# One VectorE operation a step and column in the block inverse of a gated-DeltaNet layer, with a second set of buffers, later transpositions and the decay product on VectorE

## The chip, the cores and the metric

The kernel runs on one core of one Trainium2 chip, in one launch. The metric is the device time of that launch in microseconds (us). Three runs of the kernel before took 2078.45, 2078.91 and 2074.31 us, median 2078.45. A fourth execution was taken with the hardware profiler: 2073.93 us, of which 2072.0 us are the span of its instructions. All durations below come from that execution.

## The reference, cut to what matters

One decoder block on 256 tokens of width 2048: a feed-forward part (SwiGLU, inner width 5632), a mixer, a second feed-forward part, a gated embedding and a last normalisation. The mixer is eight gated-DeltaNet heads of width 128 and sixteen state-space heads that share one input and one output projection. The change touches two places of it. The first is the inverse of a unit lower triangular matrix of each head and chunk; the second is the product of the state-space heads' decay with `cb`.

```python
lower = jnp.where(strict, jnp.einsum('bnhik,bnhjk->bnhij', kb, k) * decay, 0.0)
t_inv = lax.linalg.triangular_solve(eye + lower, eye, left_side=True, lower=True)
u = jnp.einsum('bnhij,bnhjv->bnhiv', t_inv, v * beta[..., None])
...
cb = jnp.einsum('bnlgd,bnsgd->bngls', cc, bc)
y_diag = jnp.einsum('bngrls,bnsgrp->bnlgrp', cb[:, :, :, None] * seg, xc)
```

## The kernel before, in words

**Matrix products.** Each weight tile is 128 x 2048 in float32. A DMA on SP's queue loads it (`raw`, three buffers), ScalarE casts 1024 columns of it to a rounded half `hi` (line 118), VectorE takes the rest `lo = raw - hi` (line 119), and TensorE multiplies both with the split activations. `hi` and `lo` have four buffers each. In the mixer every 1024 columns are 24 matmuls of 256 columns (lines 145 to 147: `hi` with the upper half of the activations, `hi` with the lower, `lo` with the upper). So TensorE needs one `hi` and one `lo` for each 24 matmuls, and the `lo` of VectorE stand in VectorE's one queue among all its other work.

**The mixer.** 52 input tiles (`win`) come in the order: four pairs of DeltaNet heads (k, q, v) with the state-space keys and inputs between them, then the gates z of the state-space heads, then the gates of the four DeltaNet pairs. Then 16 tiles of the output projection (`wout`) follow, which multiply `osp`, the split outputs of all heads. A gate tile pair i is multiplied into pair i's result `oT` at line 886, and casts to `osp` (lines 195 and 196) feed the output projection.

**Side work.** Everything of the heads beside the projections is written as generators (`gdn_pair`, `ssd_quad`) that go one `yield` further after each 1024 columns (`tick`). `WAIT` and `STEP` count such yields. This is only the order in which instructions are recorded; a scheduler then lays them out per engine, and every engine runs its list strictly in order.

**One pair of heads (`gdn_pair`).** Two heads and two chunks of 128 tokens make four 128 x 128 matrices. Their sixteen 32 x 32 diagonal blocks are inverted by substitution on VectorE (lines 656 to 665). Four DMAs on POOL's queue take the blocks to DRAM (line 630), one DMA on SP's queue spreads each block over eight partitions (`Lb`, line 632), and each partition solves four columns `Z`. Each of 31 steps j is two operations over all four columns: `tb` = row of L times Z's element j (line 663), then Z minus `tb` (line 665). Then `Z` goes to DRAM and back as `Y` (lines 666 and 671, POOL's queue), VectorE transposes it (line 674), and two levels of matmuls merge the blocks: `ip`, `ix`, `iy` (line 685). After them comes a chain: `y`, `st`, `o`, `ks` and `qs`, `y`, `o` (line 714), each separated by a copy on ScalarE or VectorE; then the squares on ScalarE (745), eight small POOL operations for the inverse root (747 to 751 with 220 to 225), the scaling (753), the transpositions `ot` (758) and the copy to `oT` (759). Pairs share `Lb`, `Z`, `tb`, `qs` and `o`, which have one buffer each.

**The state-space heads (`ssd_quad`).** For each of four quads POOL multiplies the decay, in two operations of 128 x 512, with `CB` (line 820). `py` (line 832) waits for that.

Of the kernel before, what the change touches and what calls it, by code (L numbers as in the profile page):

```python
# [9 lines left out]
F32 = mybir.dt.float32  # L10
F32R = mybir.dt.float32r
AF = mybir.ActivationFunctionType
ALU = mybir.AluOpType
PSUM = bass.MemoryType.PSUM

P = 128
# [27 lines left out]
BS = 32  # L44
CG = 4
# [4 lines left out]
WAIT = 4  # L50
# [18 lines left out]
def tile_hybrid_block(ctx, tc, xT, pT, con, par, wgu1, wd1, wnar, win, wout, wgu2, wd2, wproj, wple, outT):  # L69
    nc = tc.nc  # L70
    act, dve, pool, pe = nc.scalar, nc.vector, nc.gpsimd, nc.tensor
# [25 lines left out]
    def over(ap, n):  # L97
        return ap.unsqueeze(1).to_broadcast([ap.shape[0], n, ap.shape[-1]])
# [263 lines left out]
    with ExitStack() as mix:  # L362
# [213 lines left out]
        def gdn_pair(i, KQ, V):  # L576
# [16 lines left out]
            for c in range(2):  # L593
# [5 lines left out]
                for hh in range(2):  # L599
                    m = 2 * c + hh  # L600
                    dve.scalar_tensor_tensor(out=LA[:, m, 0, :], in0=ps[:, hh * T:hh * T + P], scalar=1.0, in1=ident,
                                             op0=ALU.mult, op1=ALU.mult, accum_out=ss[:, m:m + 1])
# [4 lines left out]
                              in1=beta[:, :, h0:h0 + 2], op=ALU.mult)  # L607
            for m, (c, hh) in enumerate(mats):
                dve.scalar_tensor_tensor(
                    out=LA[:, m, :, :], in0=kk[c][:, hh * T:(hh + 1) * T].rearrange("p (a i) -> p a i", a=2),  # L610
                    scalar=c1[:, m:m + 1], in1=over(d[:, c, hh, :], 2), op0=ALU.mult, op1=ALU.mult)
# [16 lines left out]
            parts = [slice(q * BS, (q + 1) * BS) for q in range(P // BS)]  # L628
            for q, p in enumerate(parts):
                nc.gpsimd.dma_start(bl.rearrange("(m b) j i -> b j m i", m=4)[q], LT[p, :, p])  # L630
            Lb = g2.tile([P, BS, BS], F32, tag="Lb", name="Lb", bufs=1)
            nc.sync.dma_start(Lb.rearrange("p j i -> p (j i)"),
                              bl.rearrange("q j i -> q (j i)").unsqueeze(1).to_broadcast([P // NG, NG, BS * BS]))
            Z = g2.tile([P, CG, BS], F32, tag="Z", name="Z", bufs=1)
            tb = g2.tile([P, CG * BS], F32, tag="tb", name="tb", bufs=1)

            Y = g2.tile([P, 4, P], F32, tag="Y", name="Y")
            pool.memset(Y, 0.0)
# [5 lines left out]
            xv = g2.tile([P, 4, P], F32, tag="xv", name="xv")  # L644
# [13 lines left out]
            for j in range(BS - 1):  # L658
                if j % STEP == 0:
                    yield  # L660
                n = BS - 1 - j
                t = tb[:, :CG * n].rearrange("p (c n) -> p c n", n=n)
                dve.tensor_tensor(out=t, in0=over(Lb[:, j, j + 1:], CG),
                                   in1=Z[:, :, j:j + 1].to_broadcast([P, CG, n]), op=ALU.mult)
                dve.tensor_tensor(out=Z[:, :, j + 1:], in0=Z[:, :, j + 1:], in1=t, op=ALU.subtract)
            nc.gpsimd.dma_start(by.rearrange("q c i -> (q c i)").rearrange("(p f) -> p f", p=P),
                              Z.rearrange("p c i -> p (c i)"))

            X = oT[:, h0:h0 + 2, :].rearrange("p n (m i) -> p (n m) i", i=P)
            for q, p in enumerate(parts):  # L670
                nc.gpsimd.dma_start(Y[p, :, p], by.rearrange("(m b) c i -> b c m i", m=4)[q])
            for _ in range(WAIT):
                yield
            dve.transpose(X, Y)

# [16 lines left out]
            S = g2.tile([P, 2, P], F32, tag="S", name="S", bufs=1)  # L692
# [21 lines left out]
                    pe.matmul(ps[:, hh * P:(hh + 1) * P], lhs[hh], rhs[:, hh, :], start=True, stop=True)  # L714
                return ps[:, 0:T].rearrange("p (h v) -> p h v", h=2)

            qs = g2.tile([P, 2, P], F32, tag="qs", name="qs", bufs=1)
            o = g2.tile([P, 4, P], F32, tag="o", name="o", bufs=1)
            y0, y1 = xv[:, 0:2, :], xv[:, 2:4, :]
            ps = two([Y[:, hh, :] for hh in range(2)], y0, "y0")  # L720
            act.copy(y0, ps)
# [9 lines left out]
            for hh in range(2):  # L731
                dve.scalar_tensor_tensor(out=y1[:, hh, :], in0=pk[:, hh, :], scalar=negc[:, h0 + hh:h0 + hh + 1],
                                         in1=y1[:, hh, :], op0=ALU.mult, op1=ALU.add)
# [28 lines left out]
        g2 = gdn_pool.enter_context(tc.tile_pool(name="g2", bufs=2))  # L762
# [20 lines left out]
        CB = mp.tile([P, 4, P], F32, name="CB")  # L783
# [15 lines left out]
        def ssd_quad(i, XS):  # L799

            g = i // 2
# [4 lines left out]
            ds = [d[:, c] for c in range(2)]  # L806
# [6 lines left out]
            for c in range(2):  # L813
                dve.tensor_tensor(out=xd[:, c], in0=ps[:, c * T:(c + 1) * T].rearrange("p (h v) -> p h v", h=4),
                                  in1=dt[:, c, h0:h0 + 4].unsqueeze(2).to_broadcast([P, 4, 64]), op=ALU.mult)
            xe = m2.tile([P, 4, 64], F32, tag="xe", name="xe", bufs=1)
            dve.tensor_tensor(out=xe, in0=xd[:, 0],
                              in1=dte[:, 8 + h0:12 + h0].unsqueeze(2).to_broadcast([P, 4, 64]), op=ALU.mult)
            for c in range(2):
                pool.tensor_tensor(out=ds[c], in0=ds[c], in1=over(CB[:, 2 * c + g, :], 4), op=ALU.mult)  # L820
            yield
            yield
            ps = mx_bank("ss0")
# [274 lines left out]
```

## Time and profile before

| what | value |
|---|---|
| three runs | 2074.31, 2078.45, 2078.91 us |
| the profiled execution | 2073.93 us; span 2072.0 us |
| TensorE busy | 2049.0 us, 99% |
| VectorE busy | 1362.2 us, 66% |
| ScalarE busy | 1035.1 us, 50% |
| POOL busy | 175.6 us, 8% |
| mixer, from its first projections to the first tile of `wout` | about 760 to 1120 us |
| substitution (lines 663 and 665) | 838 to 1059 us |

Busy time is a share over stages with different limits. TensorE is busy nearly all the time, so what can be gained or lost is the few stretches in which it is not. A line of the timeline has start, duration, engine, line, operation, output and inputs, and in brackets the idle time before it with what ended it. A line of the table of stretches has for each engine the busy time and the count of instructions, then TensorE's granted clock (1.00 is the full 2.4 GHz, 0.50 the lower level), the DMA share and GB/s.

### The profile page before, as it was taken

Reading aid. Unit: us, or ns where it says so; the run is one execution under the profiler, and the core shown is the slowest. Engines: PE = TensorE matmul, PEld = TensorE weight load, DVE = VectorE, ACT = ScalarE, POOL = GpSimd, SP = SyncE. Lnnn points to the kernel's source line nnn. Section 1 sums busy time; section 2 is a strip of 40 time slices with the busy share of each in tenths; the row PEclk is TensorE's granted clock in tenths of the full one; section 3 lists DMA queues with packets and bytes.
Section 4 is the critical chain, followed back from the end, with each engine's and each line's share of the span. In section 5 each row is a group of like instructions: output and inputs, shape, how many; then the busy total and the mean of one; then the engine's idle time right before and its main releaser. Section 6 shows DMA issues by size and latency. Waiting matters only on the chain.

```text
span 2072.0 us, 31523 instructions
## 1 busy us (share of the span) xinstructions
PE 2049.0 (99%) x12882; PEld 1832.2 (88%) x12882; DVE 1362.2 (66%) x2063; ACT 1035.1 (50%) x1544; POOL 175.6 (8%) x207
## 2 busy tenths in 40 slices
PE   9999999999999999999999999999999999999997
PEld 7888888888888889999999998888888888888886
DVE  7565555555656668999887666555555565556675
ACT  6444444444444555645545456444444444445554
POOL 2000000000000013413321111000000000000011
PEclk9999999999999999999999999999999999999998
DMA  7555555655555666554545555555556555545652
GB/s 266 190 186 183 171 176 194 211 183 183 186 184 178 197 219 218 184 179 164 162 166 173 190 179 189 190 183 184 167 184 217 182 184 185 191 162 190 208 183 102
DMA packets 64369, 384.58 MB, mean 186 GB/s; under 512 B 7616, under 2 KB 9168, under 8 KB 31072
## 3 DMA queue, kind: packets, MB, share of 16 engines
q1 hardware_dynamic: 61456, 376.75, 52.6%
q0 software_dynamic: 2480, 5.29, 0.8%
q8 instruction: 101, 1.65, 0.3%
q10 hardware_dynamic: 288, 0.52, 0.1%
q14 instruction: 44, 0.36, 0.0%
HBM read 377.78 MB, written 4.75 MB: 185 GB/s over the span
## 4 chain that ended last, share of the span: by engine, by line
PE 92%; DVE 3%; DMA 2%; issue 2%; POOL 1%; ACT 1%; POOLq 0%; DVEq 0%; SPq 0%; ACTq 0%
PE mm L130 50%; PE mm L128 24%; PE mm L146 4%; PE mm L147 4%; PE mm L145 4%; PE mm L132 1%; DVE lo L119 1%; DMA hT<-rows 1%; PE pj L130 0%; PE ip L685 0%; DMA blkl<-LA 0%; DMA blky<-Z 0%; DVE u L557 0%; PE iy L685 0%; POOL hT L820 0%
## 5 line engine op out<-in xcount | busy, mean ns | idle before, releaser
L119 DVE TENSOR_TENSOR lo<-raw,hi 128x1024 fp32r<-128x1024 f32 (+1 forms) x774 | 862.5, 1122 | 482.2 <-ACT hi L118 481.4
L130 PE MATMUL mm<-xs,hi 128*128 128x512 f32 x3088 | 1078.4, 397 | 0.7 <-DVE xs L190 0.7
L118 ACT CAST hi<-raw 128x1024 fp32r<-128x1024 f32 (+1 forms) x774 | 744.3, 963 | 558.8 <-PE mm L130 369.3
L128 PE MATMUL mm<-xs,lo 128*128 128x256 f32 x2895 | 812.7, 281 | 2.0 <-DVE lo L119 2.0
L130 PEld LDWEIGHTS mm<-xs,hi 128*128 128x128 f32 x3088 | 568.0, 188 | 124.6 <-DVE xs L190 1.2
L128 PEld LDWEIGHTS mm<-xs,lo 128*128 128x128 f32 x2895 | 543.5, 188 | 13.3 <-DVE lo L119 3.2
L130 PE MATMUL mm<-hid,hi 128*128 128x512 f32 x1408 | 492.5, 397 | 0.0
L128 PE MATMUL mm<-hid,lo 128*128 128x256 f32 x1344 | 377.8, 281 | 0.0
L130 PEld LDWEIGHTS mm<-hid,hi 128*128 128x128 f32 x1408 | 260.2, 188 | 59.0
L128 PEld LDWEIGHTS mm<-hid,lo 128*128 128x128 f32 x1344 | 253.3, 188 | 3.0
L147 PE MATMUL mm<-xs,lo 128*128 128x256 f32 x816 | 229.4, 281 | 3.4 <-DVE lo L119 3.4
L145 PE MATMUL mm<-xs,hi 128*128 128x256 f32 x816 | 229.7, 282 | 0.0
L146 PE MATMUL mm<-xs,hi 128*128 128x256 f32 x816 | 229.0, 281 | 0.0
L147 PEld LDWEIGHTS mm<-xs,lo 128*128 128x128 f32 x816 | 154.3, 189 | 4.1 <-DVE lo L119 4.0
L146 PEld LDWEIGHTS mm<-xs,hi 128*128 128x128 f32 x816 | 154.4, 189 | 0.4
L145 PEld LDWEIGHTS mm<-xs,hi 128*128 128x128 f32 x816 | 154.2, 189 | 0.6 <-issue 0.3
L168 ACT COPY t<-mm 128x256 f32<-128x256 f32 x167 | 62.2, 373 | 161.7 <-PE mm L130 160.6
L205 POOL TENSOR_TENSOR acc<-acc,sq 128x512 f32<-128x512 f32 x43 | 62.3, 1449 | 945.3 <-ACT sq L204 906.8
L169 DVE TENSOR_TENSOR t<-t,mm 128x256 f32<-128x256 f32 x167 | 69.9, 419 | 87.8 <-ACT t L168 87.5
L168 ACT COPY s<-mm 128x256 f32<-128x256 f32 x88 | 32.8, 372 | 149.0 <-PE mm L130 148.9
L169 DVE TENSOR_TENSOR s<-s,mm 128x256 f32<-128x256 f32 x88 | 37.1, 421 | 74.0 <-ACT s L168 73.9
L147 PE MATMUL mm<-osp,lo 128*128 128x256 f32 x256 | 71.8, 281 | 0.0
(304 smaller groups left out, 1444.1 us busy)
## 6 DMA issues: line engine op xcount, KB each, us to landing
raw<-in_wgu SPq DMA_DIRECT2D x173, 1024.0 KB, 4.8
raw<-in_wd SPq DMA_DIRECT2D x128, 704.0 KB, 4.1
raw<-in_win SPq DMA_DIRECT2D x52, 1024.0 KB, 4.8
raw<-in_wout SPq DMA_DIRECT2D x16, 1024.0 KB, 4.8
raw<-in_wple SPq DMA_DIRECT2D x16, 1024.0 KB, 4.8
first<-in_wgu SPq DMA_DIRECT2D x11, 256.0 KB, 7.2
hold<-hT POOLq DMA_DIRECT2D x4, 512.0 KB, 3.9
Lb<-blkl SPq DMA_DIRECT2D x4, 512.0 KB, 4.6
```

The lines of the kernel that those rows point to most:

```text
L118: act.copy(hi, src)
L119: dve.tensor_tensor(out=lo, in0=src, in1=hi.bitcast(F32), op=ALU.subtract)
L128: pe.matmul(ps[:, 0, :], lo[:, w, :], act_in[:, k, 0, :], start=False, stop=False, skip_group_check=True)
L130: pe.matmul(ps, hi[:, w, :], act_in[:, k], start=start, stop=stop, skip_group_check=True)
L132: pe.matmul(ps[:, 0, :], lo[:, w, :], act_in[:, k, 0, :], start=False, stop=False, skip_group_check=True)
L145: pe.matmul(ps[:, 0, :], hi[:, i, :], act_in[:, k, 0, :], start=k == ks[0], stop=False)
L146: pe.matmul(ps[:, 0, :], hi[:, i, :], act_in[:, k, 1, :], start=False, stop=False)
L147: pe.matmul(ps[:, 0, :], lo[:, i, :], act_in[:, k, 0, :], start=False, stop=k == ks[-1])
L168: act.copy(out, ps[:, 0, :])
L169: dve.tensor_tensor(out=out, in0=out, in1=ps[:, 1, :], op=ALU.add)
L205: pool.tensor_tensor(out=acc, in0=acc, in1=sq, op=ALU.add)
```

## The change

Five edits. Each step of the substitution becomes four operations, one for each column, that read Z's element as a scalar per partition and take the row of L times it minus the column. This turns the sign each step, so ScalarE multiplies the odd elements by -1 at the end. `tb` goes, `Lb` and `Z` get two buffers, and `qs` and `o` use the memory of `S` and `xv`. The pairs 0 to 2 yield three times more ahead of the transposition. And the product with `CB` goes from POOL to VectorE.

```diff
-            Lb = g2.tile([P, BS, BS], F32, tag="Lb", name="Lb", bufs=1)
+            Lb = g2.tile([P, BS, BS], F32, tag="Lb", name="Lb")
...
-            Z = g2.tile([P, CG, BS], F32, tag="Z", name="Z", bufs=1)
-            tb = g2.tile([P, CG * BS], F32, tag="tb", name="tb", bufs=1)
+            Z = g2.tile([P, CG, BS], F32, tag="Z", name="Z")
...
-                n = BS - 1 - j
-                t = tb[:, :CG * n].rearrange("p (c n) -> p c n", n=n)
-                dve.tensor_tensor(out=t, in0=over(Lb[:, j, j + 1:], CG),
-                                   in1=Z[:, :, j:j + 1].to_broadcast([P, CG, n]), op=ALU.mult)
-                dve.tensor_tensor(out=Z[:, :, j + 1:], in0=Z[:, :, j + 1:], in1=t, op=ALU.subtract)
+                for c in range(CG):
+                    dve.scalar_tensor_tensor(out=Z[:, c, j + 1:], in0=Lb[:, j, j + 1:], scalar=Z[:, c, j:j + 1],
+                                             in1=Z[:, c, j + 1:], op0=ALU.mult, op1=ALU.subtract)
+            odd = Z.rearrange("p c (i s) -> p c i s", s=2)[:, :, :, 1]
+            act.mul(odd, odd, -1.0)
...
-            for _ in range(WAIT):
+            for _ in range(WAIT if i == 3 else WAIT + 3):
...
-            qs = g2.tile([P, 2, P], F32, tag="qs", name="qs", bufs=1)
-            o = g2.tile([P, 4, P], F32, tag="o", name="o", bufs=1)
+            qs, o = S, xv
...
-                pool.tensor_tensor(out=ds[c], in0=ds[c], in1=over(CB[:, 2 * c + g, :], 4), op=ALU.mult)
+                dve.tensor_tensor(out=ds[c], in0=ds[c], in1=over(CB[:, 2 * c + g, :], 4), op=ALU.mult)
```

On VectorE, where the first pair's substitution starts among the splits (`lo`) and the convolutions (`u`), the list before has a product and a subtraction for each step:

```order
L557 SCALAR_TENSOR_TENSOR u<-cin,gcw,u 128x256
L663 TENSOR_TENSOR tb<-Lb,Z 128x124
L382 TENSOR_TENSOR cin<-mm,r 128x256
L665 TENSOR_TENSOR Z<-Z,tb 128x4x31
L663 TENSOR_TENSOR tb<-Lb,Z 128x120
L665 TENSOR_TENSOR Z<-Z,tb 128x4x30
```

The list now, at the same place (its lines are one lower, since the change takes a line away above):

```order
L557 SCALAR_TENSOR_TENSOR u<-cin,gcw,u 128x256
L662 SCALAR_TENSOR_TENSOR Z<-Lb,Z 128x31 x4
L382 TENSOR_TENSOR cin<-mm,r 128x256
L662 SCALAR_TENSOR_TENSOR Z<-Lb,Z 128x30 x4
L662 SCALAR_TENSOR_TENSOR Z<-Lb,Z 128x29 x4
```

Two operations a step over four columns have become four over one each: 62 for a pair have become 124, 248 in all have become 496.

On TensorE, at the end of the mixer, where the last input tile (`mm<-xs`) meets the first output tile (`mm<-osp`), the list before has nothing of a head between them:

```order
L147 MATMUL mm<-xs,lo 128x256
L145 MATMUL mm<-xs,hi 128x256
L146 MATMUL mm<-xs,hi 128x256
L147 MATMUL mm<-xs,lo 128x256
L145 MATMUL mm<-osp,hi 128x256
L146 MATMUL mm<-osp,hi 128x256
```

The list now has the last five products of the last pair of heads there:

```order
L147 MATMUL mm<-xs,lo 128x256
L714 MATMUL ks<-S,KQ 128x128 x2
L714 MATMUL qs<-S,KQ 128x128 x2
L714 MATMUL y_11171<-xv,Y 128x128 x2
L714 MATMUL o_11207<-xv,LA 128x128 x2
L758 MATMUL ot<-cont,xv 128x128 x4
L145 MATMUL mm<-osp,hi 128x256 x2
```

In the list before, these five stood further up, and 186 matmuls of input tiles lay between its `ks` and its first `mm<-osp`. Of the whole pair the merge starts later too: its `ip` stood 328 matmuls of input tiles ahead of the end, and now stands 140 ahead of it.

On POOL, in the stretch of the first pair's substitution, the list before has five products with `CB` in a row:

```order
L630 DMA blkl_6784<-LA 32x4x32 x4
L621 TENSOR_TENSOR irk<-ss,rs 128x4
L623 TENSOR_SCALAR rq<-rs 128x4
L453 TENSOR_TENSOR hT<-hT,cont 128x512
L747 TENSOR_TENSOR rq_9457<-rq 128x4
L820 TENSOR_TENSOR hT<-hT,CB 128x512 x5
L666 DMA blky_6783<-Z 128x128
```

The list now has none:

```order
L621 TENSOR_TENSOR irk<-ss,rs 128x4
L623 TENSOR_SCALAR rq<-rs 128x4
L747 TENSOR_TENSOR rq_9818<-rq 128x4
L630 DMA blkl_6784<-LA 32x4x32 x4
L453 TENSOR_TENSOR hT<-hT,cont 128x512
L666 DMA blky_6783<-Z 128x128
```

The eight products stand on VectorE's list now, two for each quad.

## Rows read from the trace of the kernel before

**Rows 1.** Stretches of the mixer: columns as told above

```profile
823.00:1080.00 257.00, 249.79 (x2159) 245.69 (x2158) 231.16 (x587) 138.66 (x258) 81.75 (x115) 0.99 0.51 175
1080.00:1150.00 70.00, 70.00 (x605) 69.71 (x604) 49.38 (x70) 38.15 (x62) 7.16 (x11) 1.00 0.50 171
```

**Rows 2.** Waits of TensorE, 740 to 1260 us: total us, times, longest

```profile
PE mm L147 <- DVE lo L119: 3.4, 3, 2.1
PE ip L685 <- DVE oT L674: 3.0, 2, 1.6
```

**Rows 3.** Stretches of 10 us around the longest of these waits

```profile
880.00:890.00 10.00, 7.94 (x54) 7.73 (x54) 9.86 (x18) 3.01 (x4) 4.09 (x4) 0.83 0.22 84
890.00:900.00 10.00, 10.00 (x90) 10.00 (x89) 9.93 (x27) 5.45 (x9) 0.61 (x1) 1.00 0.69 242
```

**Rows 4.** Timeline of POOL at the same place

```profile
876.32 7.77 POOL L820 TENSOR_TENSOR hT<-hT,CB 128x512 f32<-128x512 f32 x5 [4.88 <-DVE CB L793]
```

**Rows 5.** Timeline of VectorE at the same place

```profile
877.34 2.95 DVE L557 SCALAR_TENSOR_TENSOR u<-cin,gcw,u 128x256 f32<-128x256 f32 x2
...
884.07 1.21 DVE L119 TENSOR_TENSOR lo<-raw,hi 128x1024 fp32r<-128x1024 f32 x1
```

**Rows 6.** Groups by line, 760 to 1260 us: busy us, mean ns, idle before

```profile
L665 DVE TENSOR_TENSOR Z<-Z,tb 128x124 f32<-128x124 f32 (+30 forms) x124 | 30.4, 245 | 1.3
L663 DVE TENSOR_TENSOR tb<-Lb,Z 128x124 f32<-128x124 f32 (+30 forms) x124 | 30.3, 245 | 4.9 <-DMA Lb<-blkl 3.5
```

**Rows 7.** Timeline of VectorE, 930 to 940 us: three neighbours, start to start

```profile
931.31 0.16 DVE L603 TENSOR_SCALAR ss<-ss 128x4 f32<-128x4 f32 x1
931.38 0.16 DVE L618 TENSOR_SCALAR ss<-ss 128x4 f32<-128x4 f32 x1
...
936.45 0.34 DVE L732 SCALAR_TENSOR_TENSOR xv<-ks,negc,xv 128x128 f32<-128x128 f32 x1
936.71 0.68 DVE L561 SCALAR_TENSOR_TENSOR KQ<-th,u 128x512 f32<-128x512 f32 x1
...
939.00 0.48 DVE L557 SCALAR_TENSOR_TENSOR u<-cin,gcw,u 128x256 f32<-128x256 f32 x1
939.39 0.19 DVE L663 TENSOR_TENSOR tb<-Lb,Z 128x36 f32<-128x36 f32 x1
```

**Rows 8.** Waits of VectorE, 823 to 1080 us

```profile
DVE Z L656 <- DMA blky<-Z: 5.1, 3, 3.0
DVE tb L663 <- DMA Lb<-blkl: 3.5, 1, 3.5
```

**Rows 9.** Timeline of TensorE: one product of the last pair's chain

```profile
1098.92 0.61 PE L714 MATMUL y<-xv,Y 128*128 128x128 f32 x4
```

**Rows 10.** Timeline of VectorE: the last pair's chain

```profile
1096.21 0.61 DVE L732 SCALAR_TENSOR_TENSOR xv<-ks,negc,xv 128x128 f32<-128x128 f32 x2
...
1102.75 0.42 DVE L740 TENSOR_TENSOR o<-o,qs 128x256 f32<-128x256 f32 x1
...
1115.50 2.49 DVE L196 TENSOR_TENSOR osp<-yT,osp 128x512 fp32r<-128x512 f32 x4
```

**Rows 11.** Timeline of ScalarE: the last pair's chain

```profile
1099.57 0.37 ACT L737 COPY xv<-y 128x256 f32<-128x256 f32 x1 [1.28 <-PE y L714]
...
1103.27 0.31 ACT L745 ACTIVATE qs<-o 128x128 f32<-128x128 f32 x1 [1.79 <-DVE o L740]
...
1110.63 1.28 ACT L753 ACTIVATE o<-o,ro 128x128 f32<-128x128 f32 x4 [2.77 <-POOL ro L751]
...
1113.70 0.58 ACT L759 COPY oT<-ot 128x512 f32<-128x512 f32 x1
1114.18 2.19 ACT L195 CAST osp<-yT 128x512 fp32r<-128x512 f32 x4
```

**Rows 12.** Timeline of POOL: first and last of eight in the chain

```profile
1105.58 0.65 POOL L748 TENSOR_TENSOR rq<-rq,so 128x4 f32<-128x4 f32 x1 [15.91 <-ACT qs L745]
...
1110.40 0.20 POOL L751 TENSOR_TENSOR ro<-ro,rq 128x4 f32<-128x4 f32 x1
```

## The prediction

> **What bounds the kernel now.** I read the busy shares first: TensorE 99% of the span, VectorE 66%. The table of stretches then shows where that average hides something. From 823 to 1080 us, where the substitution lies, TensorE is busy for 249.8 of 257 us and VectorE for 231.2, so VectorE is near its limit there, and only there; in the 70 us behind it VectorE has 20.6 us free [rows 1]. The waits of TensorE say what the missing time is: three waits for a split `lo`, 3.4 us in total, and two at `ip` for the transposed `oT`, 3.0 us [rows 2]. The longest of the waits for `lo` costs more than its 2.1 us. In the ten microseconds around it TensorE ran 54 matmuls where the next ten ran 90, at a mean granted clock of 0.83, which is the lower level of 1.2 GHz for a part of it: (90 - 54) / 90 x 10 = 4.0 us, so 1.9 us are the clock [rows 3]. TensorE's work is the same matmuls in both kernels. So no edit on another engine can give more than these stalls, some 9 us of 2074, and what the change can lose is not limited in that way.
>
> **The product with `CB`.** The long wait has a visible cause. POOL ran five of the eight products in one go, 7.8 us [rows 4], and at the same time VectorE took from 877.34 to 884.07, 6.7 us, for five small operations [rows 5] of which three (convolution steps) elsewhere take 0.39 us from start to start and two (steps of the substitution) at most their duration of 0.19, 1.6 us together [rows 7]. The `lo` behind them came late and TensorE stopped. With the products on VectorE this is gone: -4.0 us. For VectorE's load it is a small gain: it lost 5.1 us in this run of five, I take 7 for all eight, and pays eight operations of 512 columns at 0.62 us, as the four splits of `osp` take 2.49 us [rows 10]: +5.0 us.
>
> **The substitution.** Before, 248 operations are busy for 60.7 us, durations that overlap their neighbours [rows 6]; counted from each start to the next start on VectorE they take about 52 us. Now 496 operations with a scalar per partition. The trace has none so short. The nearest are of the same kind with 128 and 256 columns, 0.26 and 0.39 us from start to start [rows 7], a line of 1.02 ns a column over 0.13 us; a scalar that comes with the instruction seems cheaper, as two tiny operations start 0.07 us apart [rows 7]. I take 0.13: 496 x 0.13 = 64.5 us, and for the elements, 1 + 2 + ... + 31 = 496 in each of sixteen columns (four pairs of four), 7936 at 1.04 ns, 8.3 us: 73 us, 21 us more than before. The ends: at 0.07 it is 43 us, 9 us less than before; at a whole duration, 0.34 - 0.13 = 0.21 us [rows 7], it is 112 us, 60 us more. The four columns of a step do not depend on each other, so I stay at the row of the same kind.
>
> Together VectorE gets 21 + 5 - 7 = 19 us more in a stretch in which it has 25.8 us free [rows 1]. Of these, 5.1 us are waits for `Z` to leave before its one buffer is written again, and 3.5 us a wait for `Lb` [rows 8]; both have a second buffer now, so they may become usable, but the list now has only 2 to 3 splits between a pair's last step and its transposition, where it had 4, and `Z` needs ScalarE's sign turn first, so VectorE will wait there instead. Room and need are about equal, and the last substitution ends six splits later than before, towards the emptier stretch. I charge TensorE 2 us of new waits for `lo`, between 0 (all 25.8 us usable) and 19 (none).
>
> **Buffers and transpositions.** The two waits at `ip` [rows 2] are what the three yields aim at. In the lists `ip` now stands 1.0 to 1.9 splits behind the place VectorE must have reached, before 1.5 to 2.0: a little easier for TensorE, by less than the three yields, since more VectorE work stands between two splits. I take half: -1.5 us, between 0 and -3.0. The sign turn is four short operations of ScalarE; behind each stand casts that wait with it, one cast of about 1 us a pair, and four buffered splits cover it while VectorE is ahead. Its cost is in the 2 us.
>
> **The end of the mixer.** This is the term that decides. Everything of a pair is later by what its substitution is later, and TensorE's list shows where that ends: the last pair's `ks`, `qs`, `y`, `o` and `ot` stand in one piece between the last input tile and the first output tile. They depend on each other through other engines, and TensorE has nothing else to run meanwhile. Before, 186 matmuls of input tiles lay beside this chain and no wait is recorded there. The chain by its rows in the trace of before: `ks` 0.61 (as `y`, [rows 9]), the update of `xv` 0.61 [rows 10], `y` 0.61, copy 0.37 [rows 11], `o` 0.61, sum 0.42 [rows 10], four squares at 0.31, 1.24 [rows 11], POOL's eight small operations from 1105.58 to 1110.60, 5.02 [rows 12], scaling 1.28 [rows 11], `ot` 1.1 (eight records, where `y` has four; an estimate from [rows 9]), copy to `oT` 0.58, and the first cast of `yT`, which stands behind that copy on ScalarE, a quarter of 2.19, 0.55 [rows 11]. Sum 13.0 us. Eleven handovers at about 0.05 us (1110.60 to 1110.63 is one, 1103.17 to 1103.27 another) make 0.6; VectorE's gate product and the first split of `osp` behind it hold TensorE another 0.6. That is 14.2 us, of which TensorE works for 24 records at 70 / 605 = 0.116 us [rows 1], 2.8 us that it had before as well. So 11.4 us of idle, and the lower clock behind it as in [rows 3], 1.9 us: +13.3 us. Bounds: POOL's eight at the shortest row, 0.20 us and a handover [rows 12], would take 2.2 instead of 5.0, and without the fall of the clock it is 8.6 us; nothing in the list makes it smaller.
>
> **The sum.** -4.0 - 1.5 + 2 + 13.3 = +9.8 us against the profiled execution, 2073.9 + 9.8 = 2083.7. The four executions shown lie at 2073.9, 2074.3, 2078.5 and 2078.9, so the kernel itself scatters by 0.2%; the profiled one is at the low end, 4.5 us under the median. I put the sum on the mean of the four, 2076.4, and forecast 2086 us.
>
> **Rivals.** *VectorE becomes the bound of TensorE.* For it: 231 of 257 us are busy already, and the operations double. Against it: the row of the same kind gives 0.13. It decides from about 0.13 us an operation upwards, where the free time is used up; each further 0.01 costs 5 us. At 0.16 us the substitution takes 87.7 us, VectorE has 34 us more, 17 beyond the room that is left without the 8.6 us of [rows 8]; then -5.5 + 17 + 13.3 = +25, 2101 us. If an operation held VectorE for its whole duration, 60 + 5 - 7 = 58 us more, 41 beyond the room, +49, 2125 us. The Trainium skill has a rule that would lead there ("VectorE: DVE Perf Modes", section "The DRAIN you can't avoid"): the next operation does not issue until the pipeline of the one before is empty, so that the number of operations is what to keep small. By that rule the last figure would hold. The trace does not agree: an operation of 0.16 us has its successor 0.07 us behind its start [rows 7].
>
> *Not slower: the chain at the end is short and the waits all go.* The place is the same five products. POOL's part at 2.2 us and no fall of the clock make it +8.6; all of TensorE's waits of [rows 2] with the clock go, 3.4 + 3.0 + 1.9 = -8.3, and VectorE keeps up. That is +0.3, 2077 us. For it: two of POOL's eight do take 0.20 us or less; the clock fell behind a wait of 2.1 us, but the shorter waits show no such fall. Against it: the other waits for `lo` have another cause than the `CB` products, and each of POOL's chains in the trace is some 5 us. It decides where the chain falls under 9 us.
>
> **How the numbers follow.** Chances: the forecast 0.58, with a range of its own from 2080 to 2092; VectorE as the bound 0.17; not slower 0.25. Two tenths of a per cent, 4 us, is about what a measurement of this kernel can tell from no change. The forecast and the first rival are slower by more than that; of the third case 0.15 is within it and 0.10 below, for stalls of before that the waits do not show. So faster 0.10, same 0.15, slower 0.75. The range goes from the third case on the lower runs, 2075, to the first rival at 0.16 us, 2101; it leaves the dearer part of that rival and the faster end out.
>
> **What would show it.** In the profile of the changed kernel: between the last matmul with `xs` and the first with `osp` TensorE idle for 11 us in four or five pieces, the longest of 7 to 9 us ahead of `ot`, and a granted clock of 0.5 for some microseconds behind it; no products on POOL and no VectorE operation of the convolution over 1 us beside them; line 662 with 496 operations, start to start 0.13 to 0.16 us; VectorE busy nearly without a gap from 850 to 1080 us, with waits for `Y` at its transpositions. I am wrong if that idle piece is under 6 us, or if TensorE's waits for `lo` add up to more than 10 us.

## The result and the profile after

The changed kernel takes 2103.41 us, median of four runs (2101.83 to 2104.33); the kernel before 2077.47 (2074.31 to 2078.91). The ratio is 1.0125, with a 95% interval from 1.0112 to 1.0137. So it is slower by 26 us, where the forecast was slower by 9.8 us (2086 us) and the range ended at 2101: the time lies 2 us outside it. The profiled span grew from 2072.0 to 2101.6 us, by 29.6 us, and on these two profiles the account below is made.

First the table of stretches of the changed kernel, which answers to [rows 1]:

```profile
823.00:1080.00 257.00, 240.83 (x2016) 235.89 (x2015) 247.84 (x783) 130.80 (x240) 62.50 (x92) 0.97 0.49 165
1080.00:1150.00 70.00, 61.80 (x508) 60.00 (x504) 47.90 (x108) 32.63 (x66) 14.23 (x26) 0.90 0.40 141
```

In the first stretch VectorE is busy for 247.8 of 257 us and TensorE did 2016 matmuls where it had done 2159. In the second TensorE is no longer busy throughout. Fixed stretches mislead here, since the work has shifted. So I cut both kernels at the same piece of work: from 823 us, before any substitution, to the last matmul of an input tile. The kernel before:

```profile
823.00:1117.90 294.90, 287.69 (x2489) 283.30 (x2489) 256.52 (x626) 158.88 (x297) 86.89 (x124) 0.99 0.50 171
```

The changed kernel:

```profile
823.00:1132.20 309.20, 293.03 (x2473) 287.72 (x2472) 285.71 (x872) 153.49 (x280) 74.13 (x109) 0.97 0.49 166
```

VectorE is busy for 285.7 - 256.5 = 29.2 us more and idle for 23.5 us instead of 38.4. Of the 29.2 us, then, 14.9 went into gaps, and the stretch grew by the other 14.3. That is half of the loss. In it TensorE is idle for 16.2 us where it was idle for 7.2, and busy for 5.3 us more. The other half lies behind it: the first output tile starts 12.06 us behind the last matmul of an input tile instead of 0.12, and the 16 output tiles take 93.7 us instead of 90.8, at a lower clock; together 14.9 us. From the end of the output projection on, both kernels take the same time (863.4 us before, 863.7 now).

The waits of TensorE in the changed kernel, 740 to 1290 us (total us, times, longest), which answer to [rows 2]:

```profile
PE mm L145 <- DVE Z L662: 6.3, 2, 5.7
PE ot L758 <- ACT xv L753: 5.4, 1, 5.4
PE mm L147 <- DVE lo L119: 3.6, 2, 2.0
PE yo L836 <- ACT St L826: 3.1, 1, 3.1
PE mm L145 <- DVE zt L382: 2.5, 1, 2.5
PE mm L145 <- ACT osp L195: 1.2, 1, 1.2
PE y L714 <- DVE xv L732: 1.1, 1, 1.1
```

The waits at `ip` are gone. Waits for `lo` are as long as before. New are waits of a first matmul of a tile (line 145) for VectorE: such a matmul needs a free PSUM bank (the place in which TensorE adds up a tile's sum), and in this kernel a bank is free when line 382 has taken the sum out (an eviction). The longest, in TensorE's timeline:

```profile
910.23 0.28 PE L147 MATMUL mm<-xs,lo 128*128 128x256 f32 x1
916.18 0.55 PE L145 MATMUL mm<-xs,hi 128*128 128x256 f32 x1 [5.67 <-DVE Z L662]
```

and what VectorE did meanwhile:

```profile
910.16 0.48 DVE L557 SCALAR_TENSOR_TENSOR u<-cin,gcw,u 128x256 f32<-128x256 f32 x1
910.56 0.65 DVE L662 SCALAR_TENSOR_TENSOR Z<-Lb,Z 128x5 f32<-128x5 f32 x4
911.12 1.22 DVE L119 TENSOR_TENSOR lo<-raw,hi 128x1024 fp32r<-128x1024 f32 x1
...
913.78 1.22 DVE L119 TENSOR_TENSOR lo<-raw,hi 128x1024 fp32r<-128x1024 f32 x1
914.91 0.79 DVE L662 SCALAR_TENSOR_TENSOR Z<-Lb,Z 128x4 f32<-128x4 f32 x5
915.62 0.42 DVE L382 TENSOR_TENSOR cin<-mm,r 128x256 f32<-128x256 f32 x1
915.95 0.39 DVE L662 SCALAR_TENSOR_TENSOR Z<-Lb,Z 128x24 f32<-128x24 f32 x2
```

VectorE has no gap. It makes two splits while TensorE stands still, but the eviction that frees the bank stands behind convolutions and substitution steps and ends at 916.04; TensorE starts at 916.18. The wait's name, `Z`, seems to be that of the neighbour in the list; no matmul here reads `Z`. So "how far are the splits ahead" was the wrong thing to look at: VectorE feeds TensorE in two ways, and the other one ran dry.

The lower clock costs more than it did. These pieces of the changed kernel's table of stretches are all at 0.50, 1.2 GHz; in the mixer of the kernel before there was one of 3.4 us, within [rows 3]:

```profile
836.20:839.60 3.40, 3.40 (x19) 3.40 (x18) 3.36 (x5) 3.40 (x10) 1.03 (x2) 0.50 0.37 92
914.70:921.50 6.80, 5.32 (x25) 5.35 (x26) 6.80 (x36) 1.72 (x5) 0.30 (x1) 0.50 0.43 157
1136.50:1150.20 13.70, 7.29 (x30) 6.40 (x31) 5.84 (x10) 7.29 (x21) 2.81 (x9) 0.50 0.21 77
```

Two more of 3.4 us lie at 1037.6 and 1044.4. Behind 1144.21, where the output tiles begin, 6.0 us run at half speed, which is the 3.0 us that this stage is longer.

The end of the mixer on TensorE, as forecast in one piece between the input and the output tiles:

```profile
1132.15 0.28 PE L147 MATMUL mm<-xs,lo 128*128 128x256 f32 x1
1132.27 0.60 PE L714 MATMUL ks<-S,KQ 128*128 128x128 f32 x4
...
1134.39 0.68 PE L714 MATMUL y<-xv,Y 128*128 128x128 f32 x4 [1.07 <-DVE xv L732]
1135.53 0.71 PE L714 MATMUL o<-xv,LA 128*128 128x128 f32 x4 [0.46 <-ACT xv L737]
1141.61 1.35 PE L758 MATMUL ot<-cont,xv 128*128 128x128 f32 x4 [5.37 <-ACT xv L753]
1144.21 0.77 PE L145 MATMUL mm<-osp,hi 128*128 128x256 f32 x2 [1.24 <-ACT osp L195]
```

It is idle for 8.1 us in four pieces. POOL's eight small operations, which answer to [rows 12], took 3.0 us, not 5.0:

```profile
1138.16 0.20 POOL L748 TENSOR_TENSOR rq<-rq,so 128x4 f32<-128x4 f32 x1 [9.67 <-ACT S L745]
...
1138.73 1.01 POOL L220 TENSOR_TENSOR ro<-rq,mhalf 128x4 f32<-128x4 f32 x1
...
1140.93 0.20 POOL L751 TENSOR_TENSOR ro<-ro,rq 128x4 f32<-128x4 f32 x1
```

### The profile page after: what moved, and what is told of

It is laid out like the page before. It is cut to its first block, busy times and chain, and to the rows that moved or that the text cites. A ratio compares the mean times of both kernels' runs of the same rounds, so it can differ in the third digit from the quotient of the medians.

```text
span 2101.6 us, 31806 instructions
## 1 busy us (share of the span) xinstructions
PE 2061.0 (98%) x12882; PEld 1841.8 (88%) x12882; DVE 1396.0 (66%) x2319; ACT 1035.5 (49%) x1548; POOL 164.0 (8%) x199
## 5 line engine op out<-in xcount | busy, mean ns | idle before, releaser
L128 PEld LDWEIGHTS mm<-xs,lo 128*128 128x128 f32 x2895 | 543.5, 188 | 13.3 <-DVE lo L119 3.2
L662 DVE SCALAR_TENSOR_TENSOR Z<-Lb,Z 128x31 f32<-128x31 f32 (+27 forms) x496 | 91.3, 236 | 4.7 <-DMA Lb<-blkl 4.7
```

The costliest lines, as they stand in the source:

```text
L128: pe.matmul(ps[:, 0, :], lo[:, w, :], act_in[:, k, 0, :], start=False, stop=False, skip_group_check=True)
L662: dve.scalar_tensor_tensor(out=Z[:, c, j + 1:], in0=Lb[:, j, j + 1:], scalar=Z[:, c, j:j + 1], in1=Z[:, c, j + 1:], op0=ALU.mult, op1=ALU. ...
```

## The experiments

The theory of the first four runs was that the loss has two parts that add up: new waits inside the mixer, by VectorE's load, and the five products at the end. It fell in part, and the question of the later runs was this. *The room*: VectorE's time as a whole delays TensorE and the last pair, since its idle time cannot be used as the forecast assumed. *The list*: the loss comes from where single instructions stand (the five products at the end, the evictions), or from the new operations themselves. Each kernel ran on the chip beside the kernel before, 2076.1 to 2077.0 us in these series.

### One edit taken out of the changed kernel, or made alone

Two operations a step again, all other edits kept (`u_sub`; abridged):

```diff
-                for c in range(CG):
-                    dve.scalar_tensor_tensor(...)
-            act.mul(odd, odd, -1.0)
+                dve.tensor_tensor(out=t, in0=over(Lb[:, j, j + 1:], CG), in1=..., op=ALU.mult)
+                dve.tensor_tensor(out=Z[:, :, j + 1:], in0=Z[:, :, j + 1:], in1=t, op=ALU.subtract)
```

> The changed kernel with one part undone: the substitution is again a product and a subtraction over four columns (248 operations instead of 496, no sign turn on ScalarE). Two buffers, later transpositions, the shared memory of qs and o and the CB product on VectorE stay. In its list the last pair's ks has 186 input matmuls beside it again. Theory (the number of VectorE operations causes both the new waits in the mixer and, through the list, the idle chain at its end): both go, the four us of the CB products stay gained, 2070 to 2077 us. Rival (the CB product on VectorE, the shared memory or the later transpositions cause the waits in the mixer): some 14 us of the 26 stay, 2088 to 2094 us.

Measured: 2069.75 us, ratio 0.9967 (0.9955 to 0.9979), just under the theory's range. This is faster than both kernels. All that TensorE waits for from 740 to 1290 us is

```profile
PE mm L147 <- DVE lo L119: 1.4, 2, 1.2
```

and up to the last input tile it is busy for 288.4 of 289.8 us at full clock:

```profile
823.00:1112.80 289.80, 288.36 (x2492) 283.97 (x2491) 257.47 (x633) 158.79 (x299) 77.11 (x117) 1.00 0.51 174
```

VectorE has 257.5 us of work here, 1.0 us more than in the kernel before. So the other edits add next to nothing to its load, and 28.2 of the 29.2 us are the new substitution. Measured against this kernel, which differs from the changed one by the substitution alone, less of them found a gap: the last input tile comes 19.4 us later, so 8.8 of the 28.2 us did.

The kernel before with the new substitution alone (`o_sub`; the reverse of that diff, put on the kernel before):

> The kernel before with the substitution alone changed (496 operations with a scalar per partition, sign turn on ScalarE); one buffer for Z and Lb, CB product on POOL, transpositions as before. In its list the last pair's ks has 165 input matmuls beside it. Theory (VectorE's load makes the waits in the mixer): 2090 to 2100 us, more than the changed kernel without its tail since the CB products still block VectorE. Rival (the operations fit into VectorE's free time and another edit makes the waits): 2076 to 2082 us.

Measured: 2106.68 us, ratio 1.0145 (1.0130 to 1.0161). It is 6.7 us above the theory's range. The substitution alone loses more than the whole change, without the five products at the end of its list. Up to its last input tile VectorE works 33.2 us more than in the kernel before, and the stretch is 33.0 us longer, so next to nothing found a gap:

```profile
823.00:1150.90 327.90, 296.96 (x2492) 290.65 (x2491) 289.71 (x874) 159.07 (x302) 84.92 (x125) 0.94 0.45 154
```

The two largest waits of TensorE in it:

```profile
PE ip L686 <- DVE oT L675: 12.6, 2, 11.7
PE ot L759 <- ACT o L754: 5.5, 2, 4.7
```

The changed kernel without the three yields (`u_wait`):

```diff
-            for _ in range(WAIT if i == 3 else WAIT + 3):
+            for _ in range(WAIT):
```

> The changed kernel with the three extra yields ahead of the transpositions taken away; all else as changed, with 496 operations. In its list the last pair's ks has 207 input matmuls beside it. Theory (two separate losses, 15 us at the mixer's end by the list and 14 us of waits within the mixer by VectorE's load): the first goes, the second stays, 2087 to 2092 us, and no idle piece between the last input and the first output matmul. Rival (the chain is late because VectorE is late on the chip, whatever the list): some idle piece stays there and the time is over 2096 us.

Measured: 2100.74 us, ratio 1.0119 (1.0102 to 1.0135), 2.7 us less than the changed kernel instead of some 13. The time is the rival's, over 2096 us, but no idle piece stays at the end, as the theory had said: the first output tile follows the last input tile by 0.12 us. But that last input tile comes at 1145.1 instead of 1132.1, since TensorE now stands still at a merge of the third pair:

```profile
PE ip L685 <- DVE Z L662: 16.6, 1, 16.6
PE mm L145 <- DVE Z L662: 6.2, 2, 5.6
```

VectorE's last step of the third pair lies at 1038.1 us and that pair's transposition at 1048.7, and TensorE waits from 1032.9 to 1049.6. Between the two lie the sign turn, the way through DRAM (`Z` goes out at 1039.7, `Y` is fetched from 1043.9) and 36 steps of the fourth pair, which stand ahead of the transposition in VectorE's list. So lateness of a pair is not VectorE's load alone. What was told as one theory, that the end costs 13 us of its own, has fallen. The first output tile starts at 1144.2 in the one and at 1145.2 in the other: the pairs come late, and the list only decides where TensorE waits for them.

The kernel before with the `CB` product on VectorE alone (`o_cb`; the last line of the change's diff):

> The kernel before with the CB product alone on VectorE. Theory (five POOL products in a row blocked VectorE and cost TensorE a wait of 2.1 us and 1.9 us of clock): that wait goes, 2072 to 2075 us. Rival (VectorE is at its limit and gives it back elsewhere, 5 us of products more): 2077 to 2081 us.

Measured: 2076.25 us, ratio 0.9999 (0.9990 to 1.0009). It lies between the two expectations: the long wait for `lo` is gone and 4 us do not appear. A wait at `ip` takes its place,

```profile
PE ip L685 <- DVE oT L674: 3.7, 1, 3.7
PE mm L147 <- DVE lo L119: 2.1, 2, 1.8
```

and beside it 13.7 us at the lower clock, in which 12.2 us of work take twice their time, 6 us lost:

```profile
1022.70:1036.40 13.70, 12.16 (x61) 11.54 (x62) 11.62 (x36) 3.12 (x8) 1.28 (x1) 0.50 0.33 116
```

The changed kernel with the product on POOL again (`u_cb`, the same line reversed):

> The changed kernel with the CB products back on POOL. Theory: VectorE is the bound with the new substitution, so five microseconds less work on it are worth more than the stall beside POOL's burst; 2096 to 2103 us. Rival: the move to VectorE is worth the 4 us that were forecast for it; 2104 to 2110 us.

Measured: 2103.38 us, ratio 1.0125 (1.0105 to 1.0146): no difference to the changed kernel, and between the two expectations. Waits for `lo` rise from 3.6 to 7.7 us and those at `ot` from 5.4 to 9.4, the one at `yo` (3.1 us) is gone, and those for an eviction fall from 9.4 to 7.8. With the new substitution the place of this product made no difference to the time.

### Which edits make the gain of `u_sub`

Buffers and later transpositions without the `CB` product (`o_bufwait`), buffers and the product without the later transpositions (`u_subw`), the product and the later transpositions without the buffers (`o_cbwait`); each differs from `u_sub` by one edit (abridged):

```diff
-                dve.tensor_tensor(out=ds[c], ...)                        # o_bufwait
+                pool.tensor_tensor(out=ds[c], ...)
...
-            for _ in range(WAIT if i == 3 else WAIT + 3):                # u_subw
+            for _ in range(WAIT):
...
-            Lb, Z = g2.tile(...), g2.tile(...); qs, o = S, xv            # o_cbwait
+            Lb, Z, qs, o = g2.tile(..., bufs=1), ...
```

> The kernel before with the second buffers, the shared memory of qs and o and the later transpositions, the substitution and the CB product as they were. The changed kernel with two operations a step took 2069.75 us, 7 less than before; this one differs from it by the CB product alone. If buffers and later transpositions make that gain: 2067 to 2072 us. If the CB product makes it (it does nothing by itself, 2076.25): 2074 to 2078 us.

> The changed kernel with two operations a step, and the transpositions not later than before: buffers and the CB product alone. If the later transpositions are needed for the gain of 7 us (the CB product alone left a wait of 3.7 us at ip, with 13.7 us at half clock behind it): 2073 to 2078 us. If not: 2067 to 2071 us.

> The kernel before with the CB product on VectorE and the later transpositions, all buffers as they were. If these two make the gain by themselves, since the one takes away the wait for lo and the other the wait at ip: 2067 to 2072 us. If the second buffers are needed: 2073 to 2078 us, with waits of VectorE for Z and Lb as before.

Measured: 2076.64 (ratio 1.0001, 0.9992 to 1.0011), 2079.15 (1.0015, 1.0005 to 1.0025) and 2080.11 us (1.0013, 1.0004 to 1.0023). Take any one of the three away and the gain of 7 us is gone; the first is where that was expected if the product makes the gain, and the last two come out 1 and 2 us above the higher of their expectations. Each shows another wait. Without the product's move, 4.6 us for `lo` and 2.8 at `ip`. Without the later transpositions, 7.4 us at `ip`. Without the buffers there is no wait at `ip`, but a tail:

```profile
PE ot L758 <- ACT o L753: 4.2, 1, 4.2
PE mm L147 <- DVE lo L119: 1.3, 1, 1.3
PE mm L145 <- DMA raw<-in_wout: 1.2, 1, 1.2
```

This third kernel is the cleanest price of a tail, though its buffers differ as well. Its last input tile ends at 1113.4 us, 0.6 behind that of `u_sub` (1112.7), and its `ot` and nothing else stands behind it; the first output tile starts at 1120.5 instead of 1112.8, 6.8 us then run at half clock, and the whole is 10.4 us more.

### The dose

The changed kernel with two of the four columns (`u_half`) and with three (`u_34`), which leave out a half and a quarter of the inverse:

```diff
-                for c in range(CG):
+                for c in range(CG // 2):      # u_34: range(CG - 1)
```

> The changed kernel with the substitution done for two of the four columns only (248 of the 496 new operations, half of the inverse is left out, the sign turn stays): 39 us of VectorE instead of 78. Theory: VectorE has room up to a point, some 52 us of substitution fit with 2 us of waits; under that point nothing more can be won, so 2062 to 2071 us, near the 2069.75 of two operations a step. Rival: each new operation costs TensorE its share, in proportion: halfway between 2103.4 and 2069.75 us, 2083 to 2090.

> The changed kernel with three of the four columns (372 of the 496 new operations; a quarter of the inverse is left out): about 59 us of VectorE, 7 more than two operations a step. Theory: VectorE finds some 15 us of its extra work in its gaps, and TensorE pays only what is beyond; 7 us fit, so 2068 to 2078 us, though the last product chain ends right at the first output tile in this list. Rival: the cost goes by the number of operations from 248 upwards (2073 with 248, 2103 with 496), 2086 to 2090 us.

Measured: 2073.06 us (ratio 0.9981, 0.9972 to 0.9990) and 2084.26 us (1.0035, 1.0021 to 1.0049). Both miss the theory's range, by 2 and by 6 us, and both lie under the rival's, the first by 10 us, the second by 2. So neither holds as it was put. In the first, one wait of 2.6 us for `lo` at 833 to 836 us, before the first substitution, and 3.4 us at half clock are left. In the second the last input tile ends at 1118.7 us, 0.9 later than in the kernel before but 6.0 later than in `u_sub`, which has the same other edits. Up to there VectorE is busy for 269.6 us, 12.1 more than in `u_sub`, so half of that found a gap; that 7 us more fit without a price is not shown. The rest of the loss is a tail like that of the kernel without the buffers:

```profile
PE ot L758 <- ACT xv L753: 4.2, 1, 4.2
PE mm L147 <- DVE lo L119: 3.1, 2, 1.9
PE mm L145 <- DVE zt L382: 2.4, 1, 2.4
```

I had seen this tail in the list and not priced it. The first output tile starts 7.1 us behind the last input tile, and the output tiles take 92.8 us instead of 90.8: some 9 us, near the 10.4 above.

### VectorE's time without the new operation

`u_sub` with each product issued twice:

```diff
                 dve.tensor_tensor(out=t, in0=over(Lb[:, j, j + 1:], CG), in1=..., op=ALU.mult)
+                dve.tensor_tensor(out=t, in0=over(Lb[:, j, j + 1:], CG), in1=..., op=ALU.mult)
```

> The changed kernel with the two operations a step of before, and the product of each step issued twice (the second writes the same values again). That is 372 operations of the old form and no new one; 124 of them are dead work, at some 0.21 us each 26 us of VectorE, which is what the 496 new operations cost more than the old 248 (78.5 us start to start against 52). Theory: what costs is VectorE's time in the stretch from 840 to 1060 us, whatever the form of operation; then 2095 to 2110 us, some 30 us above the same kernel without the dead products (2069.75). Rival: the new operations themselves cost, by their number, their scalar operand or the sign turn on ScalarE; then below 2088 us, of which up to 15 us would be the end of the mixer, since the last pair's chain stands alone behind the last input tile in this list as well.

Measured: 2111.66 us, ratio 1.0172 (1.0157 to 1.0187). That is 1.7 us above the theory's range and far above the rival's. 124 more operations of the old form do what 496 of the new form do: VectorE's time is enough to make the loss, and neither the scalar operand nor the sign turn is needed for it, nor does it go by the number of operations. The size does not follow from that time alone. Over the whole execution VectorE is busy for 1388.7 us here, 1396.0 in the changed kernel and 1362.6 in `u_sub`; so 26 us more of it cost 42 us here, and 33 us cost 34 there. Why is not shown. Here nearly the whole loss lies behind the last input tile (1120.1 us), where the last pair's merge has yet to be done:

```profile
PE ot L760 <- ACT xv L755: 5.4, 1, 5.4
PE ip L687 <- DVE oT L676: 4.2, 1, 4.2
```

### The evictions out of VectorE's way

```diff
-                dve.tensor_tensor(out=out[:, j, :], in0=ps, in1=r, op=ALU.mult)
+                pt = m2.tile([P, T], F32, tag="pt", name="pt", bufs=4)
+                act.copy(pt, ps)
+                dve.tensor_tensor(out=out[:, j, :], in0=pt, in1=r, op=ALU.mult)
...
-            Lb = g2.tile([P, BS, BS], F32, tag="Lb", name="Lb")
+            Lb = g2.tile([P, BS, BS], F32, tag="Lb", name="Lb", bufs=1)
```

> The changed kernel with the sums of the input tiles taken out of PSUM by ScalarE (copies to four small buffers) and multiplied by the row of scales on VectorE from there; the row blocks get one buffer again to make room. TensorE then never waits for VectorE's place in its list to get a PSUM bank. Theory one: VectorE as a whole has too much to do in the stretch; then the waits move from the banks to the splits, and the last input tile still ends at 1128 to 1140 us (1132 in the changed kernel). Theory two: the loss inside the mixer is the order of VectorE's list, the evictions standing behind the substitution; then the last input tile ends at 1113 to 1123 us and waits for a split stay under 5 us. In both the chain of the last pair stands behind the last input tile, the merge's second step included, so the whole is 5 to 10 us more than that alone: 2100 to 2120 us by the first, 2085 to 2100 by the second.

Measured: 2113.18 us, ratio 1.0177 (1.0161 to 1.0192). By the last input tile, 1115.6 us, theory two was right: with the banks freed by ScalarE, TensorE runs through its input tiles with 0.8 us of waits for `lo`, 1.3 us for a bank, and some 6 us at products of the heads. By the whole it was wrong, 13 us above its range, and the time lies in that of theory one. The largest waits, all but 1.9 us of them behind the last input tile:

```profile
PE ip L687 <- DVE oT L676: 10.9, 1, 10.9
PE ot L760 <- ACT xv L755: 7.2, 2, 5.4
```

TensorE got its tiles earlier, and then had nothing left to do while the last pair was finished. With one buffer of `Lb` less and more work on ScalarE this kernel is not the changed one in all else; how much of its 10 us more is due to that stays open.

### What the runs have in common

The last pair's transposition on VectorE (line 674; its number differs a little) says when a pair is through the substitution. In the kernel before and in the changed one (count, durations, first and last start):

```profile
L674 DVE STREAM_TRANSPOSE oT<-Y x4: 704/708/711, 909.6 to 1067.3; 128x512 f32<-128x512 f32 x4
```

```profile
L674 DVE STREAM_TRANSPOSE oT<-Y x4: 696/706/709, 930.0 to 1105.7; 128x512 f32<-128x512 f32 x4
```

| kernel | last transposition | last input tile | first output tile | median |
|---|---|---|---|---|
| two of four columns | 1047.1 | 1117.8 | 1117.9 | 2073.06 |
| buffers and later transpositions | 1057.8 | 1120.3 | 1120.4 | 2076.64 |
| two operations, all other edits | 1061.7 | 1112.7 | 1112.8 | 2069.75 |
| before | 1067.3 | 1117.8 | 1117.9 | 2077.47 |
| `CB` product alone | 1070.7 | 1121.2 | 1121.3 | 2076.25 |
| `CB` and later transpositions | 1074.1 | 1113.4 | 1120.5 | 2080.11 |
| buffers and `CB` | 1076.8 | 1122.4 | 1122.5 | 2079.15 |
| three of four columns | 1079.5 | 1118.7 | 1125.8 | 2084.26 |
| changed, without later transpositions | 1088.8 | 1145.1 | 1145.2 | 2100.74 |
| changed | 1105.7 | 1132.1 | 1144.2 | 2103.41 |
| substitution alone | 1106.2 | 1150.8 | 1150.9 | 2106.68 |
| changed, `CB` back on POOL | 1108.9 | 1134.9 | 1145.8 | 2103.38 |
| products twice | 1123.8 | 1120.1 | 1152.8 | 2111.66 |
| evictions by ScalarE | 1125.9 | 1115.6 | 1154.7 | 2113.18 |

Up to some 1070 us the first column says nothing: TensorE has input tiles enough to cover the merge and the chain behind it, and single waits make the difference. Later than that the time rises with it, with small exceptions, and not with the second column: TensorE waits in the middle for a pair or a bank, or at the end. The other edits decide which. That the pair's lateness sets the time is read from these fourteen kernels together; no run moved it alone, and a TensorE that waits can make VectorE later in its turn.

## Why the prediction failed, step by step

**The price of an operation** was right. 0.13 us and about a nanosecond a column were forecast; in the changed kernel's timeline (rows at 910.56 and 914.91 above) four of 5 columns take 0.56 us from start to start and five of 4 columns 0.71, 0.14 each. All 496 come to some 78 us, where 73 was forecast; the 5 us are six operations that took 0.6 to 1.3 us, each beside an element-wise operation of POOL (lines 453, 205 and 257). The rule that was weighed there (the Trainium skill, "VectorE: DVE Perf Modes", section "The DRAIN you can't avoid") says that the next operation does not start until the pipe of the one before has emptied, and adds that one that is not held back starts earlier. The mean duration in line 662 is 236 ns and the starts lie 0.14 us apart in the rows above, so the trace agrees with the addition and not with the bare rule.

**VectorE's room** is the step that failed. The working was: 19 us more, 25.8 us free, "room and need are about equal", a charge of 2 us. Both sides were off. The need was 29.2 us: 5 from the dearer substitution, and the 7 us back from POOL's products came to about 2 net. The stall at 877 to 884 us went, but two convolutions beside POOL's other products (line 453), which elsewhere take 0.39 us each [rows 7], took 7 us; in the kernel before a split stood at that place and took 4.9 us. VectorE's timeline of the changed kernel:

```profile
827.00 7.05 DVE L557 SCALAR_TENSOR_TENSOR u<-cin,gcw,u 128x256 f32<-128x256 f32 x2
```

And the room was half: 14.9 of the 29.2 us found a gap, measured against the kernel before (8.8 of 28.2 against `u_sub`, none in `o_sub`), and where 2 us were charged the stretch to the last input tile grew by 14.3. In the stretch from 823 to 1080 us VectorE had 9.2 us idle left, and its waits there, which answer to [rows 8], add up to nearly that:

```profile
DVE Z L662 <- DMA Lb<-blkl: 4.7, 3, 1.8
DVE lo L119 <- ACT hi L118: 2.4, 3, 1.0
DVE u L557 <- ACT u L552: 1.7, 2, 1.1
```

So VectorE stood idle for others even where it had too much to do, and that idle time was no room. The wait for `Lb` [rows 8] is still there, with two buffers: the second buffer did not bring the blocks earlier. The 5.1 us for `Z` [rows 8] did go, and the waits at the transpositions that were forecast in their place do not appear. And the end of the range of this term, 19 us, was there and was right to be there; the likeliest value should have lain near it.

**VectorE as the bound**, the first rival, is what happened, with its mechanism and, at the edge, with its condition: it was to decide from 0.13 us an operation upwards, and 78 us for the 496 are 0.14 and the columns. Its size did not follow from that. At 78 us its own working gives 26 + 5 - 7 = 24 us more, 7 beyond the room of 17.2, and some +15 us; the loss was +29.6 in the profile. Its room, the idle time less the waits of [rows 8], was near the 14.9 that found a gap. Its two errors were the 7 us back from POOL and the gains of 5.5: with the need of 29.2 us and without these gains it gives +25.

**The gains of 4.0 and 1.5 us** were not there. The waits that they were to remove, the long one for `lo` and those at `ip`, did go in the changed kernel too, and others came up: alone the `CB` product gains nothing, and on top of the new substitution nothing. It is worth 6.9 us only where the later transpositions and the buffers stand beside it, 2076.64 against 2069.75 us.

**The end of the mixer** was right in place and near in size. The +13.3 us leave out 2.8 us of work that lay among the input tiles before; cut as above, 16.1 us were forecast (14.2 of delay and 1.9 of clock) and 14.9 measured (11.9 and 3.0). In it the idle time was shorter than forecast (8.1 us for 11.4; POOL's operations took 2.0 us less) and the clock's part larger, so that the sum came so near is in part luck. But it was added as a cost of its own, that of a place in the list. Taking the place away brought back 2.7 us, so it was one of the two forms that the same lateness can take.

**The signs.** The forecast was to be wrong if the idle piece ahead of the output tiles was under 6 us, or if the waits for `lo` came to more than 10. The pieces came to 8.1 us, the longest to 5.4 where 7 to 9 was forecast, and the waits for `lo` to 3.6. So the second sign, the one for VectorE's load, did not show although that load was the failure: it looked at the splits alone, and first matmuls of tiles waited 9.4 us for evictions instead (the waits for `Z`, `zt` and `cin` at line 145).

**The sum.** Right direction, and 16 us too low against the medians, 20 against the profiles: cut as above, the stretch to the last input tile gave +14.3 where -6.3 was forecast (2 - 4.0 - 1.5, less the 2.8 us of work that moved behind it), and all else agreed within 2 us.

## What to carry to other kernels

Before counting idle time of an in-order engine as room, look at what ends each gap: what waits for another engine or a DMA stays idle, and here between none and half of the need found a place. Ask which of its results the bounding engine needs (splits, and evictions that free a bank), and when the last dependent chain starts, since here the list only chose where TensorE waited for it. Edits that each remove one wait may show nothing alone and 7 us together, because the next wait and the lower clock behind it are already there; try them together before giving one up.

## What was not expected of the hardware

The length of a spell at the lower clock did not go with the length of the wait beside it: 13.7 us at 0.50 around a wait of 3.7 us (`o_cb`), 6.8 us around one of 5.7 us and 13.7 around one of 5.4 us (the changed kernel). In such a spell a matmul of 256 columns starts every 0.21 to 0.22 us instead of 0.12 (the changed kernel at 1145 and at 1131 us). And the same eight small POOL operations took 5.0 us in the one kernel and 3.0 in the other; one of them, line 220, took 1.01 us here where its neighbours took 0.20.
